# A decoder trunk in fp32: inverse square roots moved from VectorE and ScalarE to one power instruction on GpSimd

## The chip, the cores and the metric

The kernel runs on one core of a Trainium2 chip. The metric is the device time of one launch, the median of three runs. The engines that matter are TensorE (PE, matrix products; PEld is its weight load), VectorE (DVE), ScalarE (ACT), GpSimd (POOL) and SyncE (SP, which issues most DMAs). Each engine works through its own queue in order, and an instruction that waits holds up what stands behind it on that engine.

## What is computed

Two decoder layers over 256 tokens of width 2048, then a final RMS norm, all in fp32. Layer 0 has three head groups (a gated convolution, a Mamba-2 scan, an attention into 256 memory tokens), layer 1 has two (latent attention and memory attention). What the change touches is the norm that stands in many places:

```
def rms_norm(x, w):
    y = xf * lax.rsqrt(jnp.mean(xf * xf, axis=-1, keepdims=True) + EPS)
    return (y * w.astype(jnp.float32)).astype(x.dtype)

mem_n = rms_norm(mem, mem_norm_w)
h = rms_norm(x, norm_w)                                        # both layers
y_b = y_b * lax.rsqrt(jnp.mean(y_b * y_b, axis=-1, keepdims=True) + EPS)   # layer 0, per group
q = (rms_norm(c_q, mla_q_norm_w) @ mla_w_uq)                   # layer 1
kv = (rms_norm(c_kv, mla_kv_norm_w) @ mla_w_ukv)
return rms_norm(x, final_norm_w)
```

## The kernel before

The weights stream in from HBM as a list of units; a unit is 128 or 512 output columns of one weight matrix. Each weight chunk of 128x1024 is split into a high and a low part: ScalarE casts the high part (`wh_...`, L160), VectorE subtracts it to get the low part (`wl_...`, L161), and TensorE multiplies both with activations that are split in the same way. L381 are products with a high part, L376 those with a low part; the low ones of a unit run together with those of its neighbour. L391 to L393 are the same for token-major units such as `wv`, and L627 for the packed units `dt` and `kr` (whose parts both lie in `wh_kr`, made by ScalarE in L146 and VectorE in L147).

After its products a unit has a post function. It is a generator: it does some work, yields, and is taken up again a step of the stream later. A tile scheduler then orders the instructions of each engine by priority and by what it expects them to cost, and this order is fixed in the program. High priority is given to evictions (`ev`, L397) and splits.

The inverse roots stand in three helpers. `rsqrt` (L276) works on 128x2 values: the mean plus epsilon, a bit estimate over integers, and three Newton steps. It serves the memory norm (`rcol`, value `rmc_r`), the group norms of layer 0 (`post_z`, value `grg`) and the norm of layer 1 (`post_x1`, value `r1c`). `rbcast` spreads such a column over all partitions: a diagonal `dg` on VectorE (L309), a product with ones on TensorE (`rm_pb`, L310) and a copy on ScalarE (L312). `rfull` (L315) works on 128x256 values that are already spread (a product with ones, L320): the same steps, but with a yield ahead of each Newton step. It serves x's norm in layer 0 (`r0b`) and the norms of the q and kv ranks in layer 1 (both `rc`, the last step L342 multiplies by layer 1's own root). What follows is a product with the norm's weights (L509 `hn`, L1037 `ct`) and the split into high (L346) and low half (L347).

The memory norm's root also scales the values `vm` on ScalarE (L583) and, spread as `rm`, the keys `kT` on VectorE (L581, L594). x's squares are ScalarE's (L493, L496), VectorE adds them up (L497), GpSimd folds the sum (L498), and TensorE spreads it (`r0b_ss`). Layer 1's evictions `evr` (L1007) multiply by `st["r1"]` on GpSimd.

The final norm (`post_o`, L1262) takes ScalarE's square root with the running sum as bias, a reciprocal on VectorE and one Newton step, then scales and stores five pieces of each half.

Of the kernel before, what the change touches and what calls it, by code (L numbers as in the profile page):

```python
# [204 lines left out]
def trunk_kernel(ctx, tc, a, out):  # L205
# [69 lines left out]

    def rsqrt(ssq, n, out):  # L276

        m = ssq.shape[1]
        v = tmp("nv", "nv", 2, (P, 4))[:, :m]
        V.tensor_scalar(v, ssq, 1.0 / n, EPS, ALU.mult, ALU.add)  # L280
        f = tmp("nf", "nf", 2, (P, 4))[:, :m]
        V.tensor_copy(f, v.bitcast(I32))
        V.tensor_scalar(f, f, -0.5, 1597463007.0, ALU.mult, ALU.add)
        yi = tmp("ni", "ni", 2, (P, 4), I32)[:, :m]
        V.tensor_copy(yi, f)
        y = yi.bitcast(F32)
        for i in range(3):
            V.tensor_tensor(f, y, y, ALU.mult)
            V.scalar_tensor_tensor(f, f, -0.5, v, ALU.mult, ALU.mult)
            nxt = out if i == 2 else tmp("ny", "ny", 3, (P, 4))[:, :m]  # L290
            V.scalar_tensor_tensor(nxt, f, 1.5, y, ALU.add, ALU.mult)
            y = nxt

    def rcol(accs, n, name):

# [16 lines left out]
        A.copy(rb, pb)  # L312
        return rb

    def rfull(accs, n, name, tag="rb", bufs=2, spread=True, by=None):  # L315


        ps = pat.tile([P, T], F32, name=f"{name}_ss", tag="at")
        for k, acc in enumerate(accs):
            PE.matmul(ps, ones, acc, start=k == 0, stop=k == len(accs) - 1)  # L320
        out = tmp(name, tag, bufs)
        vf = S(f"{name}_vf")
        v, f = vf[:, 0:T], vf[:, T:2 * T]
        yi = S(f"{name}_yi", I32)[:, 0:T]
        if by is None:
            V.tensor_scalar(v, ps, 1.0 / n, EPS, ALU.mult, ALU.add)
        else:
            V.scalar_tensor_tensor(v, ps, 1.0 / n, by[1], ALU.mult, ALU.mult)
            V.tensor_scalar(v, v, EPS, None, ALU.add)
        V.tensor_copy(f, v.bitcast(I32))  # L330
        V.tensor_scalar(f, f, -0.5, 1597463007.0, ALU.mult, ALU.add)
        V.tensor_copy(yi, f)
        y = yi.bitcast(F32)
        for i in range(3):
            if spread:
# [926 lines left out]
    def post_o(g):  # L1262
        def f(ps):
            gfin, xts = st["o", g]
            for i in range(2):
                xt = xts[i]
                if g == 3:
                    pre, ph = (tmp(n, n, 2, (P, 1)) for n in ("rp", "rh"))
                    V.tensor_reduce(pre, ssq[:, i, 0:3], AX.X, ALU.add)
                    V.tensor_scalar(pre, pre, 1.0 / D, EPS, ALU.mult, ALU.add)  # L1270
                for pi, (c0, p) in enumerate(ps[i]):
                    n = slice(c0, c0 + p.shape[1])
                    V.tensor_tensor(xt[:, n], p, xt[:, n], ALU.add)
                    jk = S("jk")
                    A.activation(jk[:, n], xt[:, n], AF.Square, accum_out=ssq[:, i, g + pi:g + pi + 1])
                    if g == 3 and pi + 1 == len(ps[i]):
                        V.tensor_scalar(ph, pre, -0.5, None, ALU.mult)
                    if pi + 1 < len(ps[i]):
                        V.scalar_tensor_tensor(pre, ssq[:, i, 3:4], 1.0 / D, pre, ALU.mult, ALU.add)
                    V.tensor_tensor(gfin[i][:, n], xt[:, n], gfin[i][:, n], ALU.mult)  # L1280
                x1t[i][g] = gfin[i]
                if g == 2 and i == 1:
                    A.activation(warm, ssq[:, 1, 2:3], AF.Sqrt)
                if g == 3:
                    s_ = ssq[:, i, 2 + len(ps[i]):3 + len(ps[i])]
                    v, y, z = (tmp(n, n, 2, (P, 1)) for n in ("rv", "ry", "rz"))
                    A.activation(y, s_, AF.Sqrt, scale=1.0 / D, bias=pre)
                    V.scalar_tensor_tensor(v, s_, -0.5 / D, ph, ALU.mult, ALU.add)
                    V.reciprocal(y, y)
                    V.tensor_scalar(z, y, y, v, ALU.mult, ALU.mult)  # L1290
                    r = tmp("rr", "rr", 2, (P, 1))
                    V.tensor_scalar(r, z, 1.5, y, ALU.add, ALU.mult)
                    for gg, c0, n in ((1, 0, 256), (0, 0, 512), (1, 256, 256), (3, 0, 512), (2, 0, 512)):
                        xo = x1t[i][gg][:, c0:c0 + n]
                        if gg == 0:
# [104 lines left out]
```

## Time and profile before

| | |
|---|---|
| median of three runs | 1184.31 us (1184.0 to 1185.1) |
| the profiled execution | 1183.59 us |
| its span, from the first to the last instruction | 1181.9 us |
| TensorE, weight load | 1172.1 us busy, 1017.2 us |
| VectorE, ScalarE, GpSimd | 859.7, 666.6, 83.0 us busy |
| granted TensorE clock | full, but for the last of 40 slices (0.8) |
| read from HBM, written | 220.23 MB, 4.23 MB |

The durations in the rows come from the profiled execution. Its time is 1.7 us more than the span, and 0.7 us less than the median. In a timeline a row is the start in us, the length in us, engine, line, operation, the tile written and those read, the shape, the number of merged instructions, and in brackets the idle time of the engine ahead of it with what ended that. The length of one instruction runs until its result is there; the next independent one begins a little earlier.

### The profile page before, as it was taken

What the parts mean: (1) busy time and instruction counts of PE and PEld (TensorE: products, weight loads), DVE (VectorE), ACT (ScalarE), POOL (GpSimd) and SP (SyncE); (2) the same over time, 40 slices, a digit from 0 to 9 for tenths busy, and PEclk for the clock granted to TensorE, in tenths of its full rate; (3) what the DMA queues carried; (4) which work ended last, traced back from release to release, by engine and by line L of the source; (5) the groups of instructions that cost most, each with busy time, mean ns of one, the idle gap of its engine ahead of it and who ended that gap; (6) DMA issues with size and microseconds to landing.
All of it is one profiled execution on the core that took longest, in us unless ns stands there. A gap on an engine that the chain in (4) does not pass through costs nothing.

```text
span 1181.9 us, 17221 instructions
## 1 busy us (share of the span) xinstructions
PE 1172.1 (99%) x6455; PEld 1017.2 (86%) x6455; DVE 859.7 (73%) x1592; ACT 666.6 (56%) x1195; POOL 83.0 (7%) x92
## 2 busy tenths in 40 slices
PE   9999999999999999999999999999999999999997
PEld 7888888888888898888888888889898898888886
DVE  7798897988987796666545555588766588986555
ACT  7655656666556645445444444555555587884442
POOL 0000001112000000000000000112211110110000
PEclk9999999999999999999999999999999999999998
DMA  9745646555445455555656666544554354456672
GB/s 343 268 155 208 227 162 210 182 195 188 160 172 185 147 178 199 193 187 185 216 201 214 226 214 216 176 179 165 192 184 172 108 165 139 134 187 237 230 237 98
DMA packets 45780, 225.57 MB, mean 191 GB/s; under 512 B 5473, under 2 KB 6785, under 8 KB 23425
## 3 DMA queue, kind: packets, MB, share of 16 engines
q1 hardware_dynamic: 43200, 220.88, 53.8%
q10 hardware_dynamic: 2496, 3.60, 0.9%
q8 instruction: 50, 0.82, 0.3%
q14 instruction: 34, 0.27, 0.1%
HBM read 220.23 MB, written 4.23 MB: 190 GB/s over the span
## 4 chain that ended last, share of the span: by engine, by line
PE 94%; DVE 3%; ACT 2%; issue 1%; POOL 0%; DVEq 0%; ACTq 0%; POOLq 0%
PE ps_mm L381 32%; PE ps_mm L376 17%; PE ps_tm L391 4%; PE ps_tm L393 4%; PE ps_tm L392 4%; PE ps_x L392 4%; PE ps_x L391 4%; PE ps_x L393 4%; PE ps_o L1232 3%; PE ps_o L1234 3%; PE ps_o L1233 3%; PE ps_k L607 1%; PE ps_mm L379 1%; PE py L783 1%; PE ps_k L609 1%; PE ps_pk L627 1%
## 5 line engine op out<-in xcount | busy, mean ns | idle before, releaser
L381 PE MATMUL ps_mm<-h,wh_zc 128*128 128x512 f32 x248 | 59.0, 391 | 0.0
L381 PE MATMUL ps_mm<-h,wh_xs 128*128 128x512 f32 x248 | 58.8, 391 | 0.0
L381 PEld LDWEIGHTS ps_mm<-h,wh_xs 128*128 128x128 f32 x248 | 45.9, 188 | 9.1
L381 PEld LDWEIGHTS ps_mm<-h,wh_zc 128*128 128x128 f32 x248 | 45.8, 188 | 9.1
L161 DVE TENSOR_TENSOR wl_wo<-raw_wo_2r,wh_wo 128x1024 fp32r<-128x1024 f32 x24 | 29.4, 1225 | 31.1 <-ACT wh_wo L160 31.1
L1232 PE MATMUL ps_o<-wh_wo,yl 128*128 128x512 f32 (+1 forms) x136 | 51.6, 379 | 0.0
L161 DVE TENSOR_TENSOR wl_wo<-raw_wo_1r,wh_wo 128x1024 fp32r<-128x1024 f32 x24 | 29.4, 1225 | 30.2 <-ACT wh_wo L160 30.1
L1233 PE MATMUL ps_o<-wl_wo,yl 128*128 128x512 f32 (+1 forms) x136 | 51.2, 377 | 0.0
L1234 PE MATMUL ps_o<-wh_wo,yl 128*128 128x512 f32 (+1 forms) x136 | 51.2, 377 | 0.0
L391 PE MATMUL ps_tm<-wh_z,h 128*128 128x512 f32 x128 | 51.1, 399 | 0.0
L161 DVE TENSOR_TENSOR wl_wo<-raw_wo_3r,wh_wo 128x1024 fp32r<-128x1024 f32 x24 | 29.4, 1225 | 29.5 <-ACT wh_wo L160 29.5
L391 PE MATMUL ps_x<-wh_wo,yb 128*128 128x512 f32 x128 | 50.1, 391 | 0.0
L393 PE MATMUL ps_tm<-wh_z,h 128*128 128x512 f32 x128 | 50.0, 390 | 0.0
L392 PE MATMUL ps_tm<-wl_z,h 128*128 128x512 f32 x128 | 49.8, 389 | 0.0
L393 PE MATMUL ps_x<-wh_wo,yb 128*128 128x512 f32 x128 | 49.8, 389 | 0.0
L392 PE MATMUL ps_x<-wl_wo,yb 128*128 128x512 f32 x128 | 49.8, 389 | 0.0
L401 ACT COPY s<-ps_mm 128x256 f32<-128x256 f32 x78 | 28.9, 371 | 33.0 <-PE ps_mm L376 18.4
L160 ACT CAST wh_wo<-raw_wo_1r 128x1024 fp32r<-128x1024 f32 x24 | 25.3, 1053 | 36.1 <-PE ps_x L393 19.6
L160 ACT CAST wh_wo<-raw_wo_2r 128x1024 fp32r<-128x1024 f32 x24 | 25.3, 1053 | 35.5 <-PE ps_x L393 19.6
L161 DVE TENSOR_TENSOR wl_wo<-raw_wo_0r,wh_wo 128x1024 fp32r<-128x1024 f32 x24 | 29.4, 1227 | 21.7 <-ACT wh_wo L160 20.0
L160 ACT CAST wh_wo<-raw_wo_3r 128x1024 fp32r<-128x1024 f32 x24 | 25.3, 1053 | 34.1 <-PE ps_x L393 19.6
L1026 POOL TENSOR_TENSOR cacc<-cacc,sq 128x256 f32<-128x256 f32 x8 | 9.0, 1122 | 441.2 <-ACT sq L1025 441.2
(776 smaller groups left out, 3504.0 us busy)
## 6 DMA issues: line engine op xcount, KB each, us to landing
raw_wo_0r<-in_w_out_dram SPq DMA_DIRECT2D x12, 1024.0 KB, 4.9
raw_wo_1r<-in_w_out_dram SPq DMA_DIRECT2D x12, 1024.0 KB, 4.9
raw_wo_2r<-in_w_out_dram SPq DMA_DIRECT2D x12, 1024.0 KB, 4.9
raw_wo_3r<-in_w_out_dram SPq DMA_DIRECT2D x12, 1024.0 KB, 4.8
raw_wkv0r<-in_wkv_dram SPq DMA_DIRECT2D x12, 512.0 KB, 7.2
raw_wv1r<-in_wv_dram SPq DMA_DIRECT2D x4, 1024.0 KB, 4.8
acb<-acd SPq DMA_DIRECT2D x16, 256.0 KB, 3.3
raw_z0r<-in_w_z_dram SPq DMA_DIRECT2D x4, 1024.0 KB, 4.7
```

The costliest lines, as they stand in the source:

```text
L160: i1 = self.nc.scalar.copy(h[:, e], part)
L161: i2 = self.nc.vector.tensor_tensor(l[:, e], part, h.bitcast(F32)[:, e], ALU.subtract)
L376: PE.matmul(ps[:, 0:T], wl, self.x[k][:, 0:T], start=not self.begun, stop=stop)
L379: PE.matmul(ps[:, c], wh, self.x[k][:, c], start=False, stop=False)
L381: PE.matmul(ps, wh, self.x[k], start=not self.begun, stop=stop)
L391: PE.matmul(ps[i], h, wh, start=first, stop=False)
L392: PE.matmul(ps[i], h, wl, start=False, stop=False)
L393: PE.matmul(ps[i], l, wh, start=False, stop=last)
L401: A.copy(s1[:m], ps[:m, T:2 * T])
L1232: PE.matmul(p, h, wh[:, n], start=first, stop=False)
L1233: PE.matmul(p, h, wl[:, n], start=False, stop=False)
L1234: PE.matmul(p, l, wh[:, n], start=False, stop=last)
```

## The change

Every inverse root becomes one instruction on GpSimd: `tensor_tensor` with the operation `pow`, the value as base and a column of -0.5, read with step 0, as exponent. `rsqrt` keeps its first instruction (mean plus epsilon) and loses twelve. `rfull` keeps its first one or two and loses twelve; the power stands ahead of the three yields. The final norm keeps the sums, and the square root, the reciprocal and the Newton step go, with the early load of the root's table (`warm`). The wide working tiles are one instead of two.

```
     ident = cst.tile([P, P], F32, name="ident")
     make_identity(nc, ident)
+    mhalf = cst.tile([P, 1], F32, name="mhalf")
+    G.memset(mhalf, -0.5)
...
     def rsqrt(ssq, n, out):
-        m = ssq.shape[1]
-        v = tmp("nv", "nv", 2, (P, 4))[:, :m]
+        v = tmp("nv", "nv", 2, (P, 4))[:, :ssq.shape[1]]
         V.tensor_scalar(v, ssq, 1.0 / n, EPS, ALU.mult, ALU.add)
-        f = tmp("nf", "nf", 2, (P, 4))[:, :m]
-        V.tensor_copy(f, v.bitcast(I32))
-        V.tensor_scalar(f, f, -0.5, 1597463007.0, ALU.mult, ALU.add)
-        yi = tmp("ni", "ni", 2, (P, 4), I32)[:, :m]
-        V.tensor_copy(yi, f)
-        y = yi.bitcast(F32)
-        for i in range(3):
-            V.tensor_tensor(f, y, y, ALU.mult)
-            V.scalar_tensor_tensor(f, f, -0.5, v, ALU.mult, ALU.mult)
-            nxt = out if i == 2 else tmp("ny", "ny", 3, (P, 4))[:, :m]
-            V.scalar_tensor_tensor(nxt, f, 1.5, y, ALU.add, ALU.mult)
-            y = nxt
+        G.tensor_tensor(out, v, mhalf[:, 0:1].to_broadcast([P, ssq.shape[1]]), ALU.pow)
...
-    def rfull(accs, n, name, tag="rb", bufs=2, spread=True, by=None):
+    def rfull(accs, n, name, tag="rb", bufs=2, by=None):
...
-        V.tensor_copy(f, v.bitcast(I32))
-        V.tensor_scalar(f, f, -0.5, 1597463007.0, ALU.mult, ALU.add)
-        V.tensor_copy(yi, f)
-        y = yi.bitcast(F32)
-        for i in range(3):
-            if spread:
-                yield
-            V.tensor_tensor(f, y, y, ALU.mult)
-            V.scalar_tensor_tensor(f, f, -0.5, v, ALU.mult, ALU.mult)
-            V.scalar_tensor_tensor(out, f, 1.5, y, ALU.add, ALU.mult)
-            y = out
+        G.tensor_tensor(out, v, mhalf.to_broadcast([P, T]), ALU.pow)
+        for _ in range(3):
+            yield
         if by is not None:
             V.tensor_tensor(out, out, by[0], ALU.mult)
...
-                if g == 2 and i == 1:
-                    A.activation(warm, ssq[:, 1, 2:3], AF.Sqrt)
                 if g == 3:
                     s_ = ssq[:, i, 2 + len(ps[i]):3 + len(ps[i])]
-                    v, y, z = (tmp(n, n, 2, (P, 1)) for n in ("rv", "ry", "rz"))
-                    A.activation(y, s_, AF.Sqrt, scale=1.0 / D, bias=pre)
-                    V.scalar_tensor_tensor(v, s_, -0.5 / D, ph, ALU.mult, ALU.add)
-                    V.reciprocal(y, y)
-                    V.tensor_scalar(z, y, y, v, ALU.mult, ALU.mult)
-                    r = tmp("rr", "rr", 2, (P, 1))
-                    V.tensor_scalar(r, z, 1.5, y, ALU.add, ALU.mult)
+                    v, r = (tmp(n, n, 2, (P, 1)) for n in ("rv", "rr"))
+                    V.scalar_tensor_tensor(v, s_, 1.0 / D, pre, ALU.mult, ALU.add)
+                    G.tensor_tensor(r, v, mhalf, ALU.pow)
```

Since the scheduler lays the program out anew, other instructions change places too. The line numbers of the changed kernel are smaller by 20 in the middle of the file (L342 is L322 there, L161 stays).

The first place is the early part of ScalarE, where the memory norm ends and x's squares begin (`vm` is scaled by the root `rmc_r`, `ea` is an exponential, `xacc` the first square). Before:

```order
L496 ACTIVATE sq_725<-x_7_442 128x512
L401 COPY s_729<-ps_mm 128x256
L160 CAST wh_wk_2_0_733<-raw_wk_2r_650 128x1024
L160 CAST wh_wk_2_1024_739<-raw_wk_2r_650 128x1024
L160 CAST wh_wk_3_0_790<-raw_wk_3r_737 128x1024
L401 COPY s_786<-ps_mm 128x256
L160 CAST wh_wk_3_1024_796<-raw_wk_3r_737 128x1024
L583 ACTIVATE vm_0_140<-vm_0_140,rmc_r 128x512
L583 ACTIVATE vm_1_141<-vm_1_141,rmc_r 128x512
L312 COPY rm<-rm_pb 128x256
L489 ACTIVATE ea<-ea 128x64
```

Now:

```order
L381 COPY s_623<-ps_k_199 128x256
L563 ACTIVATE vm_0_142<-vm_0_142,rmc_r 128x512
L563 ACTIVATE vm_1_143<-vm_1_143,rmc_r 128x512
L469 ACTIVATE ea<-ea 128x64
L473 ACTIVATE xacc<-x_0_430 128x512
L476 ACTIVATE sq_694<-x_1_432 128x512
L476 ACTIVATE sq_697<-x_2_434 128x512
```

The two multiplications of `vm` and the exponential have moved from behind the squares and three splits to ahead of the first square.

The second place is VectorE at the norm of the q rank in layer 1 (`rc_v` and `rc` are its value and root, `ct` the weighted rows, `cqHL` their halves, `wl_ckv` low parts of the weights that come next). Before:

```order
L337 TENSOR_TENSOR rc_vf<-rc 128x256
L161 TENSOR_TENSOR wl_ckv_0_7602<-raw_ckv3r_7550,wh_ckv_0_7601 128x1024
L338 SCALAR_TENSOR_TENSOR rc_vf<-rc_vf 128x256
L402 TENSOR_TENSOR crkv_7540<-ps_mm,s_7595 128x256
L339 SCALAR_TENSOR_TENSOR rc<-rc_vf,rc 128x256
L161 TENSOR_TENSOR wl_ckv_1024_7608<-raw_ckv3r_7550,wh_ckv_1024_7607 128x1024
L337 TENSOR_TENSOR rc_vf<-rc 128x256
L338 SCALAR_TENSOR_TENSOR rc_vf<-rc_vf 128x256
L339 SCALAR_TENSOR_TENSOR rc<-rc_vf,rc 128x256
L342 TENSOR_TENSOR rc<-rc,r_7219 128x256
L1037 SCALAR_TENSOR_TENSOR ct<-crq_7229,cols,rc 128x256 x2
L147 TENSOR_TENSOR wh_kr_7686<-raw_krr_7605,wh_kr_7686 128x8x64
```

Now:

```order
L316 SCALAR_TENSOR_TENSOR rc_v<-rc_ss,r1sq 128x256
L382 TENSOR_TENSOR crkv_7437<-ps_mm,s_7438 128x256
L317 TENSOR_SCALAR rc_v<-rc_v 128x256
L161 TENSOR_TENSOR wl_ckv_1024_7450<-raw_ckv2r_7388,wh_ckv_1024_7449 128x1024
L322 TENSOR_TENSOR rc<-rc,r_7119 128x256
L1017 SCALAR_TENSOR_TENSOR ct<-crq_7129,cols,rc 128x256 x2
L327 TENSOR_TENSOR cqHL_7522<-ct,cqHL_7522 128x256
L327 TENSOR_TENSOR cqHL_7527<-ct,cqHL_7527 128x256
L1017 SCALAR_TENSOR_TENSOR ct<-crq_7228,cols,rc 128x256 x2
L161 TENSOR_TENSOR wl_ckv_0_7493<-raw_ckv3r_7447,wh_ckv_0_7492 128x1024
L382 TENSOR_TENSOR crkv_7437<-ps_mm,s_7486 128x256
L161 TENSOR_TENSOR wl_ckv_1024_7499<-raw_ckv3r_7447,wh_ckv_1024_7498 128x1024
```

The root is used right behind one split, and both splits of the unit `ckv3` and all of `wh_kr` now stand behind it; before, they stood between the steps.

The third place is VectorE at the norm of the kv rank (`wl_mq` and `wl_mz` are low parts of the next units, `zc` a gate, `evr` an eviction). Before:

```order
L329 TENSOR_SCALAR rc_vf<-rc_vf 128x256
L330 CAST rc_vf<-rc_vf 128x256
L331 TENSOR_SCALAR rc_vf<-rc_vf 128x256
L332 CAST rc_yi<-rc_vf 128x256
L411 SCALAR_TENSOR_TENSOR zc_7848<-zs_th,zh 128x256
L337 TENSOR_TENSOR rc_vf<-rc_yi 128x256
L338 SCALAR_TENSOR_TENSOR rc_vf<-rc_vf 128x256
L339 SCALAR_TENSOR_TENSOR rc<-rc_vf,rc_yi 128x256
L161 TENSOR_TENSOR wl_mz_0_0_7933<-raw_mz_0r_7856,wh_mz_0_0_7932 128x1024
L405 SCALAR_TENSOR_TENSOR evr<-ps_mm,s_7925 128x256
L337 TENSOR_TENSOR rc_vf<-rc 128x256
L161 TENSOR_TENSOR wl_mz_0_1024_7939<-raw_mz_0r_7856,wh_mz_0_1024_7938 128x1024
```

Now:

```order
L161 TENSOR_TENSOR wl_mq_0_1024_7741<-raw_mq_0r_7678,wh_mq_0_1024_7740 128x1024
L317 TENSOR_SCALAR rc_v<-rc_v 128x256
L391 SCALAR_TENSOR_TENSOR zc_7730<-zs_th,zh 128x256
L322 TENSOR_TENSOR rc<-rc,r_7119 128x256
L1017 SCALAR_TENSOR_TENSOR ct<-crkv_7437,cols,rc 128x256 x2
L161 TENSOR_TENSOR wl_mz_0_0_7809<-raw_mz_0r_7738,wh_mz_0_0_7808 128x1024
L385 SCALAR_TENSOR_TENSOR evr<-ps_mm,s_7801 128x256
L327 TENSOR_TENSOR ckvHL_7781<-ct,ckvHL_7781 128x256
L327 TENSOR_TENSOR ckvHL_7786<-ct,ckvHL_7786 128x256
L1017 SCALAR_TENSOR_TENSOR ct<-crkv_7567,cols,rc 128x256 x2
L391 SCALAR_TENSOR_TENSOR zc_7730<-zs_th,zh 128x256
L161 TENSOR_TENSOR wl_mz_0_1024_7815<-raw_mz_0r_7738,wh_mz_0_1024_7814 128x1024
```

The instruction that reads the root (L342, now L322) stood behind both splits of `mz` and the first of `zc`; now it stands ahead of the first split of `mz`.

Elsewhere: on TensorE `rm_pb` has moved ahead by a unit, behind the low products of `wk_0`, and `r0b_ss` by four products; on VectorE the five multiplications of keys by `rm` and an eviction have moved in between the adds of x's squares. The order on SyncE's queue is the same.

## Rows read from the trace of the kernel before

**Rows 1.** The page: busy us (share) and instructions; the chain that ended last, by engine.

```profile
PE 1172.1 (99%) x6455; PEld 1017.2 (86%) x6455; DVE 859.7 (73%) x1592; ACT 666.6 (56%) x1195; POOL 83.0 (7%) x92
...
PE 94%; DVE 3%; ACT 2%; issue 1%; POOL 0%; DVEq 0%; ACTq 0%; POOLq 0%
```

**Rows 2.** Groups of instructions on GpSimd: name, shape, count | busy us, mean ns | idle.

```profile
L1051 POOL TENSOR_TENSOR uqrr<-rop,rop 128x256 f32<-128x256 f32 x8 | 5.9, 737 | 15.4 <-DVE rop L1048 15.4
L790 POOL TENSOR_TENSOR xsd<-xsd,yo 128x512 f32<-128x512 f32 x4 | 5.3, 1336 | 13.2 <-DVE yo L788 13.2
```

**Rows 3.** Timeline of ScalarE, 51 to 65 us: start, length, what.

```profile
51.28 0.64 ACT L493 ACTIVATE xacc<-x 128x512 f32<-128x512 f32 x1
...
62.85 1.33 ACT L583 ACTIVATE vm<-vm,rmc_r 128x512 f32<-128x512 f32 x2 [0.31 <-DVE rmc_r L291]
64.09 0.36 ACT L312 COPY rm<-rm_pb 128x256 f32<-128x256 f32 x1
```

**Rows 4.** Timeline of VectorE, 52 to 66 us.

```profile
52.69 0.68 DVE L497 TENSOR_TENSOR xacc<-xacc,sq 128x512 f32<-128x512 f32 x1
...
58.76 0.68 DVE L497 TENSOR_TENSOR xacc<-xacc,sq 128x512 f32<-128x512 f32 x1
...
64.51 0.42 DVE L326 TENSOR_SCALAR r0b_vf<-r0b_ss 128x256 f32<-128x256 f32 x1
64.85 1.42 DVE L581 TENSOR_TENSOR kT<-kT,rm 128x256 f32<-128x256 f32 x4
```

**Rows 5.** Timeline of GpSimd, 41 to 61 us.

```profile
41.40 1.65 POOL L479 TENSOR_TENSOR macc<-macc 128x256 f32<-128x256 f32 x1 [10.86 <-DVE macc L477]
59.58 1.68 POOL L498 TENSOR_TENSOR xacc<-xacc 128x256 f32<-128x256 f32 x1 [16.52 <-issue]
```

**Rows 6.** Timeline of TensorE, 57 to 74 us.

```profile
57.59 5.40 PE L381 MATMUL ps_mm<-memHL,wh_wk 128*128 128x512 f32 x23
63.35 0.68 PE L310 MATMUL rm_pb<-dg,ones 128*128 128x128 f32 x4 [0.36 <-DVE dg L309]
63.87 0.60 PE L320 MATMUL r0b_ss<-xacc,ones 128*128 128x256 f32 x2
...
70.23 3.59 PE L381 MATMUL ps_mm<-memHL,wh_wk 128*128 128x512 f32 x15
73.66 0.39 PE L391 MATMUL ps_tm<-wh_wv,memHL 128*128 128x512 f32 x1
```

**Rows 7.** Timeline of VectorE at the kv norm, 804 to 810 us.

```profile
804.11 1.71 DVE L161 TENSOR_TENSOR wl_mq<-raw_mq_0r,wh_mq 128x1024 fp32r<-128x1024 f32 x1
805.75 0.28 DVE L329 TENSOR_SCALAR rc_vf<-rc_vf 128x256 f32<-128x256 f32 x1
...
808.52 1.22 DVE L161 TENSOR_TENSOR wl_mz<-raw_mz_0r,wh_mz 128x1024 fp32r<-128x1024 f32 x1
```

**Rows 8.** Timeline of VectorE at the q norm, 774 to 787 us.

```profile
774.40 0.42 DVE L328 SCALAR_TENSOR_TENSOR rc_vf<-rc_ss,r1sq 128x256 f32<-128x256 f32 x1
...
784.29 0.42 DVE L342 TENSOR_TENSOR rc<-rc,r 128x256 f32<-128x256 f32 x1
784.75 0.88 DVE L1037 SCALAR_TENSOR_TENSOR ct<-crq,cols,rc 128x256 f32<-128x256 f32 x2
785.55 0.68 DVE L147 TENSOR_TENSOR wh_kr<-raw_krr,wh_kr 128x512 fp32r<-128x512 f32 x1
786.15 0.75 DVE L347 TENSOR_TENSOR cqHL<-ct,cqHL 128x256 fp32r<-128x256 f32 x2
```

**Rows 9.** Timeline of TensorE, the products with `kr` and the low ones with `mz`.

```profile
790.87 3.82 PE L627 MATMUL ps_pk<-h,wh_kr 128*128 128x512 f32 x16
...
811.63 2.08 PE L376 MATMUL ps_mm<-h,wl_mz 128*128 128x256 f32 x16
```

**Rows 10.** Timeline of VectorE behind the last matmul.

```profile
1175.10 0.16 DVE L1288 SCALAR_TENSOR_TENSOR rv<-ssq,rh 128x1 f32<-128x1 f32 x1
...
1176.18 1.41 DVE L1298 TENSOR_SCALAR gf<-gf,rr 128x256 f32<-128x256 f32 x4
```

More of the change, by code (lines that the diff above doesn't have):

```diff
@@ L321, in rfull @@
         out = tmp(name, tag, bufs)
-        vf = S(f"{name}_vf")
-        v, f = vf[:, 0:T], vf[:, T:2 * T]
-        yi = S(f"{name}_yi", I32)[:, 0:T]
+        v = S(f"{name}_v")[:, 0:T]
         if by is None:
@@ L1267, in f @@
                 if g == 3:
-                    pre, ph = (tmp(n, n, 2, (P, 1)) for n in ("rp", "rh"))
+                    pre = tmp("rp", "rp", 2, (P, 1))
                     V.tensor_reduce(pre, ssq[:, i, 0:3], AX.X, ALU.add)
@@ L1275, in f @@
                     A.activation(jk[:, n], xt[:, n], AF.Square, accum_out=ssq[:, i, g + pi:g + pi + 1])
-                    if g == 3 and pi + 1 == len(ps[i]):
-                        V.tensor_scalar(ph, pre, -0.5, None, ALU.mult)
                     if pi + 1 < len(ps[i]):
```

## The prediction, made before the changed kernel was run

> **What bounds the kernel now.** I began with the busy times: TensorE is busy for 99% of the span, VectorE for 73%, ScalarE for 56% and GpSimd for 7% [rows 1]. The chain that ended last agrees: 94% of it is TensorE [rows 1]. So work taken off VectorE buys nothing by itself; only what makes TensorE wait, or what stands behind its last matmul, counts. In the timeline TensorE waits visibly for one thing that the change touches, the diagonal of the memory norm: its issue would have come at 57.59 + 23 x 0.229 = 62.86 (the pace is that of 15 matmuls from 70.23 to 73.66) and came at 63.35 [rows 6], so 0.5 us. Behind the last matmul the chain of the final norm runs from 1175.10 to 1176.18 [rows 10]. These two places, 1.6 us, are all that the change can win.
>
> **What it removes.** Each of the six short roots (`rsqrt`) loses 12 VectorE instructions, each of the three wide ones (`rfull`) 12, and the tail 8. All of it but the two places above lies beside a saturated TensorE: value 0. What hides it is TensorE's own work, and that cover stays.
>
> **What it adds.** Eleven powers on GpSimd: three of 128x256, six of 128x2, two of 128x1. No row shows a power. The nearest are GpSimd's two-input passes: 737 ns for 256 columns and 1336 ns for 512 [rows 2], so 599 ns per 256 columns and 138 ns fixed. One bound is a single pass, 0.74 us. The other: a power is a logarithm, a product and an exponential; the logarithm that this kernel writes out (lines 647 to 656) takes 18 instructions, an exponential taken as long makes 36 steps, and 0.138 + 36 x 0.599 = 21.7 us. I take 12 steps, the number that the removed chain needs for the same root: 0.138 + 12 x 0.599 = **7.3 us** for a wide power, and 0.2 us for a short one. That lies nearer to the pass than to the series, and it is the weakest number here.
> [...]
>
> **What it moves.** The built order was laid out as if the power were short, and this decides the price: the waiting instruction stands early in an in-order queue, with work for TensorE behind it.
>
> *Early, x's norm.* The two multiplications of `vm` now stand ahead of the squares: these begin 1.33 us later [rows 3], VectorE's adds at 52.69 + 1.33 = 54.0 [rows 4]. Up to the last add VectorE now runs 7 adds of 0.69, six 128x256 steps of about 0.36 (four times `kT` by `rm`, and two more) and one split of 1.22 [rows 4, 7]: 8.2 us, so 62.2. GpSimd's own add ends 0.14 + 1.68 later [rows 4, 5]: 64.0. TensorE's sum `r0b_ss` stands four matmuls earlier and `rm_pb` (0.52) now ahead of it: 62.86 - 4 x 0.229 + 0.52 = 62.5 [rows 6]. It waits 1.5, against the 0.5 that `rm_pb` no longer waits (VectorE makes its diagonal ahead of the adds now, and its turn comes behind a whole unit's low products). Since VectorE overlaps instructions by some hundredths, the net is +0.6 to +1.1; **+0.9**. The wide power after it begins near 64.0 + 0.6 + 0.4 + 0.1 = 65.1 (the distance from 63.87 to 64.51 and the length of L326 [rows 4, 6]) and ends at 72.4. The first `hn` (0.5) and the split `wl_wv_0` (1.22) follow: 74.2. TensorE wants the split one matmul behind 73.66, which is 74.8 after the delay. **0**; above 8 us of power it costs the excess.
>
> *The q norm.* Value ready at 774.40 + 0.42 + 0.36 + 0.28 = 775.5 [rows 7, 8], power until 782.9. Behind it on VectorE, before the first half of `wh_kr` is done: L342 0.46, three pairs of `ct` at 0.88, three pairs of low halves at 0.75, two splits of 1.22, one eviction 0.36 and the half itself 0.68 [rows 7, 8]; 8.8 us, less some overlap, plus two hand-overs to ScalarE's casts of about half a microsecond. So about 792, where TensorE wants it at 790.87 [rows 9]. **+1.0**; it begins at 6.3 us of power.
>
> *The kv norm.* Here VectorE has least ahead. Value ready at 805.75 + 0.28 = 806.03 [rows 7], hand-over 0.14, power, then L342 0.46, two `ct` 0.80 and the split `wl_mz_0_0` 1.22 [rows 7, 8]: 808.7 plus the power. TensorE wants it at 811.63 [rows 9]. Slack 2.9 us, so a wait of 7.3 - 2.9 = 4.4. The second half of that split now has an eviction, two low halves, two `ct` and a `zc` ahead of it: 0.36 + 0.75 + 0.88 + 0.36 + 1.22 = 3.6 [rows 4, 7, 8], some 3.3 with the overlap, while TensorE eats the first in half of 2.08 [rows 9]. Another 2.3. **+6.7**. In the kernel before the same split was ready at 809.7, behind only part of the chain; the steps were spread so that none of them blocked it.
>
> *Short powers in the middle.* In the four group norms VectorE waits about 0.4 us ahead of a split, where one is prepared well before its use: 0. In layer 1's norm TensorE's broadcast also stands earlier than before, a few matmuls behind the value: 0, and the excess if a short power costs over half a microsecond.
>
> *Tail.* The square root, reciprocal and two steps go; from 1175.10 [rows 10]: 0.16 for `rv`, 0.14 hand-over, 0.17 power, 0.03 back, so 1175.6 instead of 1176.18: **-0.6**. If a short power were as slow as GpSimd's slowest pass here, 1.68 [rows 5], it would be +0.9. ScalarE's table load for the root goes too; it was hidden: 0. The DMA queues keep their order.
>
> **Sum.** +0.9 + 0 + 1.0 + 6.7 - 0.6 = +8.0 us. The profiled execution took 1183.59 with a span of 1181.9, which makes 1191.6; the median of the three runs lies 0.7 above it, 1184.31, which makes **1192.3**. At one pass per power: +0.9 - 0.6 = +0.3, 1184.6. At 21.7 us: 0.9 + 13.7 + 15.4 + 21.1 - 0.6 = +50.5, 1235. A split beside a busy GpSimd took 1.71 instead of 1.22 [rows 7]; if every power slowed VectorE so, the early place could add 1 to 3 us.
>
> **Rivals.**
> 1. *The power is short, under 4 us: not slower.* The kv slack of 2.9 us covers nearly all of it, and the early wait and the shorter tail cancel: 1184.6, up to 1186.5 near 4 us. For it: a pass costs 0.74 [rows 2]. Against it: a root to full accuracy in five passes or less, where the removed chain needed 12. Chance 0.28.
> 2. *The power is a long series or runs nearly element by element, over 14 us.* All three places then pay nearly in full: from 1184.31 + 27 = 1211 at 14 us, 1235 at 21.7, 1260 at 30 and beyond. Chance 0.20.
> 3. *The first power pays once.* It is that of the memory norm, and ScalarE's `vm` multiplications and with them all squares wait for it. [...] Against it: GpSimd's first pass of the program, like its second, shows 1.7 us and no such stretch [rows 5]. Chance 0.06. [...]
> 4. *Faster.* The early sum comes in time after all and the tail shortens: -0.5 - 0.6 = -1.1, 1183.2. More cannot come, since TensorE has no other wait to lose. Faster by over 0.2% would need twice that. Chance 0.03.
>
> **How the numbers follow.** A difference of 0.2%, 2.4 us, is about what a measurement of this kernel can tell from none. The forecast (a power of 4 to 14 us) has 0.43, and gives 1186.5 to 1211. Slower: 0.43 + 0.20 + 0.06, less 0.01 at the 4 us edge, 0.68. Same: 0.28 + 0.01, and 0.01 of rival 4, 0.30. Faster: 0.02. The range goes from 1184.0, which leaves out the lower part of rival 1 and rival 4, to 1240, a power of about 23 us, which leaves out the far part of rival 2: together about 0.17.
>
> **What would show it.** GpSimd's rows for the new line `rfull` writes with: 7 us each, and under 0.3 us for the short ones. VectorE idle ahead of `rc` with GpSimd as releaser, about 7 us at both places of layer 1. TensorE: waits at the low products of `mz` after 811 (4.4 and 2.3), at `wh_kr` (1.0) and at `r0b_ss` (1.5), none at `rm_pb`. A wide power under 3 us, or over 14, makes the number wrong and leaves the places right; a wait of TensorE anywhere else makes the reasoning wrong.

## The result: 117 us slower, and the profile after

The changed kernel takes 1301.19 us (median of five runs, 1299.19 to 1302.07) against 1184.31: a ratio of 1.098, interval 1.0966 to 1.0993. The forecast was 1192.3 with a range up to 1240, so the sign was right and the size wrong by a factor of fifteen. The span of the profiled execution grew from 1181.9 to 1298.3 us, by 116.4.

The page of the changed kernel: busy times, granted clock in 40 slices, and the chain that ended last.

```profile
PE 1178.7 (91%) x6455; PEld 1021.8 (79%) x6455; DVE 838.0 (65%) x1476; ACT 666.6 (51%) x1191; POOL 207.9 (16%) x104
...
PEclk9967999999999999999999999776699999999999
...
PE 82%; POOL 10%; DVE 3%; ACT 2%; issue 1%; DMA 1%; POOLq 0%; DVEq 0%; ACTq 0%
```

Against [rows 1], VectorE has lost 21.7 us of work and GpSimd has gained 124.9. TensorE is as busy as before but for 6.6 us, and stands still for 8% more of a longer span. GpSimd, 0% of the chain before, is now 10% of it: 125 us in three pieces. Among the longest pieces of that chain (start, length, what) they stand out:

```profile
65.39 41.27 POOL r0b L318
...
811.26 42.11 POOL rc L318
879.90 41.25 POOL rc L318
```

One power of 128x256 takes 41.3 us, the second of them 42.1. The prediction took 7.3; the upper of its two bounds was 21.7, and its second rival was priced up to 30. Why the second one is longer is not shown by a run of its own. It began 0.1 us behind the start of a split on VectorE (811.14 to 812.37), while at the beginning of the other two no split was running. The short ones, by groups of instructions on GpSimd (form, count | busy, mean ns | idle before):

```profile
L282 POOL TENSOR_TENSOR grg<-nv,mhalf 128x2 f32<-128x2 f32 x4 | 2.8, 708 | 26.5 <-DVE nv L281 26.5
L1264 POOL TENSOR_TENSOR rr<-rv,mhalf 128x1 f32<-128x1 f32 x2 | 1.1, 560 | 119.8 <-DVE rv L1263 119.8
L282 POOL TENSOR_TENSOR rmc_r<-nv,mhalf 128x2 f32<-128x2 f32 x1 | 0.7, 729 | 7.4 <-DVE nv L281 7.4
```

What TensorE waited for in the changed kernel (total us, times, longest):

```profile
PE ps_mm L356 <- DVE wl_mz L161: 41.7, 2, 40.0
PE ps_mm L361 <- ACT wh_ckv L160: 33.0, 1, 33.0
PE ps_tm L372 <- DVE wl_wv L161: 33.0, 1, 33.0
PE r0b_ss L310 <- POOL xacc L478: 1.1, 1, 1.1
PE ps_pk L607 <- DVE wh_kr L147: 1.1, 1, 1.1
```

The three large waits belong to the three wide powers, one each. VectorE reads the root, waits for it, and holds up a split behind it:

```profile
65.56 2.77 DVE L161 TENSOR_TENSOR wl_wk<-raw_wk_3r,wh_wk 128x1024 fp32r<-128x1024 f32 x2
106.69 0.48 DVE L489 SCALAR_TENSOR_TENSOR hn<-x,cols,r0b 128x256 f32<-128x256 f32 x1 [38.36 <-POOL r0b L318]
107.09 1.22 DVE L161 TENSOR_TENSOR wl_wv<-raw_wv1r,wh_wv 128x1024 fp32r<-128x1024 f32 x1
```

At the q norm the split that TensorE misses first is ScalarE's. ScalarE's queue holds the cast of `cqHL`, which needs VectorE's `ct`, ahead of the second cast of `ckv3`:

```profile
812.09 1.05 ACT L160 CAST wh_ckv<-raw_ckv3r 128x1024 fp32r<-128x1024 f32 x1 [0.65 <-PE ps_mm L361]
854.37 0.80 ACT L326 CAST cqHL<-ct 128x256 fp32r<-128x256 f32 x2 [41.23 <-DVE ct L1017]
855.08 1.04 ACT L160 CAST wh_ckv<-raw_ckv3r 128x1024 fp32r<-128x1024 f32 x1
```

So one slow instruction blocks three queues in turn: GpSimd's, VectorE's (41.0 us) and ScalarE's (41.2). TensorE here works on weights that are already split for 11.9 us from the start of the power, then stands until 2.8 us behind its end: 42.1 - 11.9 + 2.8 = 33.0.

After each of these waits TensorE is also slower. Stretches of the changed kernel (from:to, length, busy us and instructions of PE, PEld, DVE, ACT, POOL, granted clock, DMA share, GB/s):

```profile
108.36:111.87 3.51, 3.51 (x8) 2.82 (x9) 3.44 (x8) 1.00 (x3) 0.00 (x0) 0.52 0.30 65
111.87:116.00 4.13, 4.13 (x20) 3.39 (x19) 4.13 (x10) 2.90 (x6) 0.00 (x0) 1.00 0.48 198
...
923.70:926.00 2.30, 2.08 (x8) 1.78 (x8) 2.30 (x6) 1.53 (x3) 0.84 (x1) 0.50 0.00 0
926.00:929.60 3.60, 2.09 (x10) 2.09 (x10) 3.60 (x6) 2.14 (x5) 0.00 (x0) 0.50 0.33 57
```

Behind the 33 us at `wl_wv` the granted clock is 0.52 (108.36 to 111.87), and eight products take 3.51 us instead of 8 x 0.229 = 1.83: 1.7 us. TensorE at the other two places:

```profile
856.17 3.53 PE L361 MATMUL ps_mm<-h,wh_ckv 128*128 128x512 f32 x8 [33.04 <-ACT wh_ckv L160]
859.54 2.06 PE L356 MATMUL ps_mm<-h,wl_ckv 128*128 128x256 f32 x16
...
923.71 2.08 PE L356 MATMUL ps_mm<-h,wl_mz 128*128 128x256 f32 x8 [39.98 <-DVE wl_mz L161]
927.51 2.08 PE L356 MATMUL ps_mm<-h,wl_mz 128*128 128x256 f32 x8 [1.72 <-DVE wl_mz L161]
...
933.80 3.80 PE L361 MATMUL ps_mm<-h,wh_zc 128*128 128x512 f32 x16
```

At the q norm eight products take 859.54 - 856.17 = 3.4 instead of 1.83, at a granted clock of 0.53 (856.20 to 859.50): 1.5 us. At the kv norm, at 0.50 up to 929.6 and 0.72 from there to 932, it is 10.1 us from the first low product of `mz` to the next unit, of which 1.7 is the second wait. Before, it was 5.6, from 811.63 [rows 9] to this row of the same view:

```profile
817.21 1.07 PE L381 MATMUL ps_mm<-h,wh_zc 128*128 128x512 f32 x4
```

That leaves 2.8 us for the clock. The account: waits of 33.0 + 33.0 + 1.1 + 41.7 = 108.8, clock 1.7 + 1.5 + 2.8 = 6.0, `r0b_ss` 1.1, less the 0.4 that `rm_pb` no longer waits [rows 6] and 0.25 in the tail. That is 115.3 of the 116.4 us.

This account says how TensorE spent its time, not what a full clock would have given back. VectorE finishes the first half of `wh_kr` at 862.65, and its work from the root on waits for TensorE nowhere:

```profile
861.96 0.69 DVE L147 TENSOR_TENSOR wh_kr<-raw_krr,wh_kr 128x512 fp32r<-128x512 f32 x1
```

So at full clock TensorE would have been 1.5 us earlier at `wh_kr` and would have waited 1.5 us longer there. In the same way the first eight low products of `mz`, 2.08 us instead of 1.04, fill 1.0 us of the time until the second half of the split is there. By these rows, and no run tests it with the clock held up, the slow clock itself costs about 1.7 + 1.8 = 3.5 us; the other 2.5 belong to VectorE's path.

The tail, VectorE behind the last product: from `rv` to the first scaling 1292.62 - 1291.79 = 0.83 us, where it was 1.08 [rows 10].

```profile
1291.79 0.16 DVE L1263 SCALAR_TENSOR_TENSOR rv<-ssq,rp 128x1 f32<-128x1 f32 x1
1292.62 1.41 DVE L1270 TENSOR_SCALAR gf<-gf,rr 128x256 f32<-128x256 f32 x4 [0.67 <-POOL rr L1264]
```

### The profile page after: what moved, and what is told of

It is laid out like the page before. It is cut to its first block, busy times and chain, and to the rows that moved or that the text cites. A ratio compares the mean times of both kernels' runs of the same rounds, so it can differ in the third digit from the quotient of the medians.

```text
span 1298.3 us, 17105 instructions
## 1 busy us (share of the span) xinstructions
PE 1178.7 (91%) x6455; PEld 1021.8 (79%) x6455; DVE 838.0 (65%) x1476; ACT 666.6 (51%) x1191; POOL 207.9 (16%) x104
## 4 chain that ended last, share of the span: by engine, by line
PE 82%; POOL 10%; DVE 3%; ACT 2%; issue 1%; DMA 1%; POOLq 0%; DVEq 0%; ACTq 0%
PE ps_mm L361 27%; PE ps_mm L356 15%; POOL rc L318 6%; PE ps_tm L372 4%; PE ps_tm L371 4%; PE ps_tm L373 4%; PE ps_x L372 4%; PE ps_x L371 4%; PE ps_x L373 4%; POOL r0b L318 3%; PE ps_o L1212 3%; PE ps_o L1214 3%; PE ps_o L1213 3%; PE ps_k L587 1%; PE ps_mm L359 1%
## 5 line engine op out<-in xcount | busy, mean ns | idle before, releaser
L318 POOL TENSOR_TENSOR rc<-rc_v,mhalf 128x256 f32<-128x256 f32 x2 | 83.3, 41670 | 5.2 <-DVE rc_v L317 5.2
L356 PE MATMUL ps_mm<-h,wl_mz 128*128 128x256 f32 x128 | 18.7, 302 | 41.7 <-DVE wl_mz L161 41.7
L741 POOL TENSOR_TENSOR m<-m,cbT 128x512 f32<-128x512 f32 x16 | 22.7, 1423 | 211.1 <-ACT m L738 137.7
L322 DVE TENSOR_TENSOR rc<-rc,r 128x256 f32<-128x256 f32 x2 | 0.9, 426 | 82.0 <-POOL rc L318 82.0
L356 PEld LDWEIGHTS ps_mm<-h,wl_mz 128*128 128x128 f32 x128 | 17.6, 208 | 42.4 <-DVE wl_mz L161 42.2
L161 DVE TENSOR_TENSOR wl_wo<-raw_wo_2r,wh_wo 128x1024 fp32r<-128x1024 f32 x24 | 29.4, 1225 | 31.0 <-ACT wh_wo L160 31.0
L161 DVE TENSOR_TENSOR wl_wo<-raw_wo_1r,wh_wo 128x1024 fp32r<-128x1024 f32 x24 | 29.4, 1225 | 30.2 <-ACT wh_wo L160 30.1
L161 DVE TENSOR_TENSOR wl_wo<-raw_wo_3r,wh_wo 128x1024 fp32r<-128x1024 f32 x24 | 29.4, 1225 | 29.6 <-ACT wh_wo L160 29.6
```

Of the source, the lines that this page charges most:

```text
L161: i2 = self.nc.vector.tensor_tensor(l[:, e], part, h.bitcast(F32)[:, e], ALU.subtract)
L318: G.tensor_tensor(out, v, mhalf.to_broadcast([P, T]), ALU.pow)
L356: PE.matmul(ps[:, 0:T], wl, self.x[k][:, 0:T], start=not self.begun, stop=stop)
L741: G.tensor_tensor(m4, m4, cb.unsqueeze(1).to_broadcast([P, 2, 2, P]), ALU.mult)
```

## Experiments

The theory after this profile (A): a power on GpSimd costs by its columns, 0.41 us and 0.15 to 0.16 for each (an estimate from 0.56 us for one column, 0.71 for two and 41.3 for 256), and the three of 256 columns, with the queues behind them, make the whole loss. Rivals: the short powers and the new order cost something of their own (B); the place of the waiting instructions matters, not the length of the power (C); a busy GpSimd slows VectorE or TensorE (E).

### The wide roots back on VectorE, and the wide roots alone

The first kernel is the changed one with the old `rfull`; the second is the kernel before with the new `rfull` only.

```
-        G.tensor_tensor(out, v, mhalf.to_broadcast([P, T]), ALU.pow)
-        for _ in range(3):
-            yield
+        V.tensor_copy(f, v.bitcast(I32))
...
+        for i in range(3):
+            if spread:
+                yield
+            V.tensor_tensor(f, y, y, ALU.mult)
...
```

> The changed kernel, with the three wide roots back as Newton steps on VectorE; the eight short powers and the tail stay. Theory A (the three 41 us powers of 128x256, 161 ns per column, and the queues held behind them make the whole loss): the 117 us go, 1184.0 to 1184.6, the tail 0.2 to 0.3 us shorter (rv to first gf 0.83 instead of 1.08 us). Rival B (the short powers, 0.56 to 0.73 us each, and the new order of the program cost something of their own): 1186 or more, with new TensorE waits at rm_pb, at the broadcast of r1c or at the group norms.

Measured: 1184.33 us against 1184.67 for the kernel before on the same chip, ratio 0.9997 (0.9989 to 1.0006).

> The kernel before, with only the three wide roots as powers on GpSimd; short roots and tail stay Newton steps. Theory A: all of the loss stands here, 1300 to 1302, with TensorE waits of 33, 33 and 40 us and no others over 2 us. Rival B: some us less than 1301, and what is missing belongs to the short powers.

Measured: 1302.37 us, ratio 1.0993 (1.0978 to 1.1008); TensorE's large waits are 41.8, 33.9 and 33.0 us, and nothing else is over 0.4 but the 1.1 at the start that stood there before. So theory A holds: the loss is that of the three wide powers, and the eight short ones with the tail cost and win nothing that the time shows. B falls.

### The wide root on two columns

The sums are taken as a column of 128x2, the power works on that, and the column is spread as the memory norm's is.

```
+        pc = pat.tile([P, 2], F32, name=f"{name}_ss", tag="at")
+        for i in range(2):
+            for k, acc in enumerate(accs):
+                PE.matmul(pc[:, i:i + 1], acc[:, i * P:(i + 1) * P], ones[:, 0:1], ...)
...
-        G.tensor_tensor(out, v, mhalf.to_broadcast([P, T]), ALU.pow)
+        G.tensor_tensor(r, v, mhalf.to_broadcast([P, 2]), ALU.pow)
...
+        out = rbcast(r, name, tag, bufs)
```

> The changed kernel, with each wide root taken on a column of 128x2 (sums by products with one column of ones) and spread afterwards by a diagonal and a product with ones, as the memory norm does. Theory A (a power costs by its columns, 0.41 + 0.15 per column): the three powers take 0.7 us, and the time is 1184 to 1186. Rival C (what costs is the place: a root on another engine's queue, waited for early in VectorE's order): over 1190, whatever the width.

Measured: 1187.13 us, ratio 1.0024 (1.0014 to 1.0033). The same three roots in the same places, by the view of that line: length in ns (least, median, most), first and last start.

```profile
L319 POOL TENSOR_TENSOR rc_r<-rc_v,mhalf x2: 699/700/701, 776.3 to 801.0; 128x2 f32<-128x2 f32 x2
L319 POOL TENSOR_TENSOR r0b_r<-r0b_v,mhalf x1: 823/823/823, 64.5 to 64.5; 128x2 f32<-128x2 f32 x1
```

41.3 us have become 0.7 to 0.8, and 114 of the 117 us are back: the width decides, and C falls as the whole cause. The time is 1.1 us above what I expected: TensorE is busy for 1173.8 us instead of 1172.1, since the column needs 18 more products than the spread value (6473 instead of 6455), and it still waits 1.1 us at `r0b_ss`. This form is slower than Newton's steps on the spread value.

### Powers that nobody reads

```
+            powers = [(P, 1), (P, 16), (P, 64), (P, 128), (P, T), (32, T), (32, 64)] if g == 0 else [(P, T)] * 2
+            for m, c in powers if g < 2 else ():
+                pw = tmp("pw", "hn", 2)[:m, 0:c]
+                G.tensor_tensor(pw, three[:m].to_broadcast([m, c]), mhalf[:m].to_broadcast([m, c]), ALU.pow)
```

> The kernel before, plus twelve powers on GpSimd of constants, read by nobody, in the stretch where GpSimd has nothing else to do: 128x1, 128x16, 128x64, 128x128, 128x256 (three times), 32x256, 32x64 with base 3 and exponent -0.5, and 128x64 with base 1, with exponent 3 and with exponent 1. Theory A: the length is 0.41 + 0.16 per column, so 2.9, 10.6, 20.8 and 41.3 us, the same for 32 partitions as for 128, and for every exponent; nobody waits, so the time is that of before, 1184 to 1185, and the splits on VectorE beside a power take 1.22 us as else. Rival E (a busy GpSimd slows VectorE or TensorE): some 270 us of powers lengthen the splits beside them, and the time goes over 1187.

Measured: 1226.96 us, ratio 1.0362 (1.0348 to 1.0376). The groups on GpSimd:

```profile
L969 POOL TENSOR_TENSOR pw<-three,mhalf 128x256 f32<-128x256 f32 x3 | 124.8, 41608 | 0.2
L969 POOL TENSOR_TENSOR pw<-three,mhalf 32x256 f32<-32x256 f32 x1 | 41.6, 41609 | 0.1
L969 POOL TENSOR_TENSOR pw<-three,mhalf 128x128 f32<-128x128 f32 x1 | 20.7, 20728 | 0.1
L973 POOL TENSOR_TENSOR pw<-ones,mhalf 128x64 f32<-128x64 f32 x1 | 10.5, 10517 | 0.1
L973 POOL TENSOR_TENSOR pw<-three,ones 128x64 f32<-128x64 f32 x1 | 10.5, 10516 | 0.1
L969 POOL TENSOR_TENSOR pw<-three,mhalf 128x16 f32<-128x16 f32 x1 | 3.6, 3568 | 0.1
L969 POOL TENSOR_TENSOR pw<-three,mhalf 128x1 f32<-128x1 f32 x1 | 0.6, 578 | 215.9 <-DVE ya L351 215.9
```

The price is (41.608 - 0.578) / 255 = 0.161 us per column, whether 128 partitions or 32 take part (41.6 us for both on 256 columns; 10.5 and 11.0 on 64), whether the base is 3 or 1, and whether the exponent is -0.5 or 1; base 3 with exponent 3 takes the same 10.5 us on 64 columns. A column of GpSimd's two-input pass costs 0.599 / 256 = 0.0023 us [rows 2], so a power is worth about 69 passes.

Rival E falls, too, as far as such powers go. While the first nine ran without a gap from 560 to 774, VectorE's splits of the output weights took what they take in the kernel before, here those of one unit, by the view of that line over 561 to 770 us in both kernels, the run with powers first:

```profile
L161 DVE TENSOR_TENSOR wl_wo<-raw_wo_1r,wh_wo x14: 1224/1225/1226, 609.3 to 645.6; 128x1024 fp32r<-128x1024 f32 x14
```

```profile
L161 DVE TENSOR_TENSOR wl_wo<-raw_wo_1r,wh_wo x14: 1224/1225/1227, 609.4 to 645.6; 128x1024 fp32r<-128x1024 f32 x14
```

So a split did not wait for a power: 1225 ns beside it and 1225 without it. These powers read one column again and again, and the powers of the changed kernel a whole tile; but there, too, the two splits at 65.56 ran to their end beside the power of 65.39 to 106.66, in 2.77 us together, where a pair takes 2.35 at 928.05.

The time was missed, by an accident that taught something: the powers began only at 560, behind a value of VectorE, and the last ended at 805.7, when layer 1's sums of squares were waiting on GpSimd. Nobody read a power, and TensorE lost 40.8 us all the same, and 1.8 more in the 16 low products behind the wait (3.7 us, 809.10 to 812.77, where 16 take 1.9 in the kernel before, 811.63 to 813.55; during the wait, from 774 to 805, the granted clock was 0.50):

```profile
PE ps_mm L380 <- DVE wl_ckv L161: 40.8, 1, 40.8
```

ScalarE's next square (the squares have two buffers) waited 48.8 us for GpSimd's sum of an earlier one, and the casts of `ckv` stood behind that square. A power costs by what is queued behind it, not only by who reads it.

### The readers moved late

```
+            tc.keep_in_program_order(V.tensor_tensor(out, out, by[0], ALU.mult))
...
-        for _ in range(3):
+        for _ in range(3 + late):
...
-CK_LAG = 3
+CK_LAG = 8
```

with `late` 12 at the q and kv norm, 0 at x's norm.

> The changed kernel, in which the instructions that read the q and the kv root are pinned twelve steps of the stream later instead of three, and the kv norm itself five steps later; their results are first used some 100 us after the root begins. The root of x's norm stays as it is. Rival C (only the place of the waiting instructions on VectorE costs): both waits of layer 1 go, about 75 us and the slow clock after them, 1221 to 1226. Theory A with GpSimd's queue (it works in order as well, and while it is at a power, layer 1's scalings by r1, the rope and the sums of squares stand behind it, ScalarE behind those and TensorE behind ScalarE): only a part is won, 1235 to 1285, and TensorE's waits move to casts of ScalarE that follow GpSimd.

Measured: 1280.4 us, ratio 1.0812 (1.0793 to 1.0832). What TensorE waited for in layer 1 (the 33.0 us behind x's norm stay), and below it ScalarE:

```profile
PE ps_mm L356 <- DVE wl_zc L161: 57.4, 2, 36.6
```

```profile
ACT zs_th L389 <- POOL zh L990: 69.1, 19, 37.5
...
ACT sq L1005 <- POOL cacc L1006: 26.8, 1, 26.8
```

VectorE no longer waits for a root in layer 1, and 20.8 us are won out of the 75.8 that were to be had there. The rest has moved to GpSimd's queue: the squares of the kv rank (26.8 us, which stops TensorE for 20.8) and the scaled gates `zh` (37.5, which stops it for 36.6) stand behind a power, ScalarE stands behind them, and the casts behind ScalarE. GpSimd serves this stage every few us (from 782 to 897 in the kernel before its longest idle time is 8.8 us), so 41 us on it find no hole.

### The size that the prediction assumed

```
-        G.tensor_tensor(out, v, mhalf.to_broadcast([P, T]), ALU.pow)
+        G.tensor_tensor(out, v, v, ALU.mult)
+        G.tensor_tensor(out[:, 0:38], v[:, 0:38], mhalf.to_broadcast([P, 38]), ALU.pow)
```

> The changed kernel with the size that my prediction assumed: each wide root is a GpSimd product over all 256 columns (0.74 us) and a power over the first 38 (0.41 + 38 x 0.161 = 6.5), 7.3 us together; 218 columns of each root hold the square of the value and not its root. If the places and the slacks of the prediction are right and only the duration was wrong: +0.9 early, nothing at hn, +1.0 at kr, +6.7 at mz's low products (4.4 and 2.3), -0.25 tail, so 1192 to 1193. If the queues behind ScalarE's casts, which the prediction did not follow, decide at this size too: 1195 or more, with a wait of TensorE at casts of ckv.

Measured: 1198.78 us, ratio 1.0124 (1.011 to 1.0138), so 14.9 us over the kernel before, not 8. The pieces took 8.1 us together at x's and the q norm and 7.2 at the kv norm. TensorE's waits and its path through `mz`:

```profile
PE ps_mm L357 <- DVE wl_mz L161: 7.7, 2, 5.9
PE ps_pk L608 <- DVE wh_kr L147: 1.8, 1, 1.8
PE r0b_ss L310 <- POOL xacc L479: 1.1, 1, 1.1
...
PE ps_tm L373 <- DVE wl_wv L161: 0.2, 1, 0.2
```

TensorE's timeline at the kv norm:

```profile
821.19 2.08 PE L357 MATMUL ps_mm<-h,wl_mz 128*128 128x256 f32 x8 [5.94 <-DVE wl_mz L161]
824.99 2.08 PE L357 MATMUL ps_mm<-h,wl_mz 128*128 128x256 f32 x8 [1.72 <-DVE wl_mz L161]
...
832.21 3.80 PE L362 MATMUL ps_mm<-h,wh_zc 128*128 128x512 f32 x16
```

The value of the kv norm on VectorE, and the stretch of TensorE behind the first wait, columns as above:

```profile
811.02 0.28 DVE L317 TENSOR_SCALAR rc_v<-rc_v 128x256 f32<-128x256 f32 x1
```

```profile
821.00:824.00 3.00, 2.08 (x8) 1.78 (x8) 3.00 (x8) 2.23 (x5) 0.84 (x1) 0.50 0.00 0
```

The places are those of the prediction, with no wait at a cast of `ckv`: ScalarE's queue decided only at the longer power (33.0 us at 42.1, none at 8.1). The waits come to 7.7 (for 6.7), 1.8 (for 1.0), 1.1 (for 1.5) and 0.2 (for 0). The largest part of what is over that is the clock: from 821.19 to 832.21 it takes 11.0 us, where the kernel before took 5.6; less the wait of 1.7 that is 3.7 us, at a granted clock of 0.50 up to 828 and 0.69 from there to 832, after a wait of only 5.9. As above, 1.0 of it fills time in which TensorE would have waited for the second half of `mz`. Behind the 1.8 us at `wh_kr` the granted clock is 1.00 (794 to 798).

The first wait is 5.9 us and not 7.2 - 2.9 = 4.3, because the value comes later. TensorE wants the low part of `mz` at 821.19 - 5.94 = 815.25, 4.2 us behind the start of L317; before it was 811.63 - 805.75 = 5.9 [rows 7, 9]. The trace shows where this comes from: ScalarE copies out the packed product `kr`, on which this chain of VectorE and GpSimd rests, 5.8 us behind its first matmul (794.18 to 800.00) and not 3.9 (790.87 to 794.72), since what stood behind the q norm's root has piled up ahead of it.

### A version that is under both

In the changed kernel `r0b_ss` waits 1.1 us. To see whether the scalings of `vm` and `kT` ahead of x's squares cause it, they were pinned behind x's norm, in the kernel with Newton's steps for the wide roots:

```
-        for k in ks:
-            V.tensor_tensor(k, k, st["rm"], ALU.mult)
-        for i in range(2):
-            A.mul(vm[0][i], vm[0][i], st["rmc"][:, i:i + 1])
         x_square()
         yield
         yield
         yield from x_norm()
+        for k in ks:
+            tc.keep_in_program_order(V.tensor_tensor(k, k, st["rm"], ALU.mult))
+        for i in range(2):
+            tc.keep_in_program_order(A.mul(vm[0][i], vm[0][i], st["rmc"][:, i:i + 1]))
```

> As the run with Newton steps for the wide roots, and the scalings of vm and kT by the memory norm's root are pinned behind x's norm instead of standing ahead of x's squares. If these scalings are what makes r0b_ss late (1.1 us in the changed kernel), that wait goes: 1183.0 to 1183.5, 0.1% under both kernels or nearly so. If the wait comes from elsewhere (the short power before the squares, GpSimd's add), it stays, 1184.3.

Measured: 1182.76 us against 1184.06, ratio 0.9990 (0.9981 to 0.9999). All waits of TensorE that are left:

```profile
PE warm_ps L243 <- DVE wz L240: 1.1, 1, 1.1
PE ps_lt L1156 <- DVE pl L1149: 0.3, 1, 0.3
```

The time is 0.2 us below the range that I gave. `r0b_ss` waits no longer, so the scalings were the cause; `rm_pb` does not wait either, as in the changed kernel. Three controls and a repetition ask which part wins. The tail's power alone, in the kernel before:

> The kernel before, with only the final norm's root as a power of 128x1. From 1.08 to 0.83 us between rv and the first scaling: 0.25 us less, 1184.1, too little to tell from no change by the time alone; my prediction had -0.6. Rival: ScalarE's square root was hidden beside VectorE's own step and the handovers to GpSimd cost as much, then 0.

Measured: 1184.18 against 1184.67, ratio 0.9995 (0.9986 to 1.0004). The place of the scalings alone, without any power:

> The kernel before, without any power, with the scalings of vm and kT pinned behind x's norm as in the run at 1182.76. If the short powers and the tail's power give that run its gain (no wait at rm_pb, 0.4 to 0.5 us, and 0.25 us in the tail): 1184.0 as before, with the wait at rm_pb still there. If the place of the scalings alone gives it: 1182.8 to 1183.3.

Measured: 1184.34 against 1183.92, ratio 1.0002 (0.9993 to 1.0011). Beside it, on the same chip, the version again:

> The same kernel as e7_scale_late, beside the control without powers on one chip: 1182.5 to 1183.3, under the kernel before by 0.05 to 0.15%.

Measured: 1182.89, ratio 0.9990 (0.9981 to 0.9999). With the late scalings, short powers without the tail's, and the tail's without the short ones:

> The kernel at 1182.8 (short powers, tail's power, scalings behind x's norm, wide roots as Newton steps) with the final norm's root back as square root, reciprocal and Newton step. If its gain comes from the short powers and the order they bring (no TensorE wait at rm_pb): 1183.0 to 1183.3, only the tail's 0.25 us given back. If it comes from the tail: 1184.0 or more.

Measured: 1183.53 against 1184.13, ratio 0.9994 (0.9985 to 1.0003), which lies between the two cases and decides for neither.

> The control without powers (1184.34) with the tail's power alone: 0.25 us less if the tail is worth what its chain shows, 1184.1, with the wait at rm_pb of 0.4 us still there; under 1183.5 if the tail gives most of the gain.

Measured: 1184.29, ratio 1.0000 (0.9991 to 1.0009); `rm_pb` waits 0.4 us there.

Only both parts together, with the late scalings, can be told from the kernel before, by 0.1%, twice, and both times the interval ends just short of 1. The short power for the memory norm takes away the wait at `rm_pb`, and the tail's chain is 0.25 us shorter; the rest of the 1.0 to 1.3 us lies within what single runs differ by, and which part gives it stays open.

## Why the prediction was wrong, and where it was right

**What failed: the price of a power.** "I take 12 steps, the number that the removed chain needs for the same root: 0.138 + 12 x 0.599 = 7.3 us for a wide power" is the step, and the 36 steps that make 21.7 are the bound above it. A wide power is worth 69 passes, and takes 41.3 to 42.1 us. Neither the removed chain nor a written-out logarithm says how GpSimd makes a power, and how it does stays open. The short one was mis-sized by the same step: 0.70 to 0.73 and 0.56 us for 0.2. The range ended at a power of 23 us, so it could not hold the result.

**What held: the places, and two of the three thresholds.** Put 41.3 us into the prediction's own sums: 41.3 - 8 = 33.3 behind x's norm, 41.3 - 6.3 = 35.0 at the q norm, 41.3 - 2.9 + 2.3 = 40.7 at the kv norm. The waits are 33.0; 33.0 and 1.1 together 34.1; and 41.7. At the assumed size a power of 8.1 us cost 0.2 behind x's norm (threshold 8) and 1.8 at the q norm (threshold 6.3). At the q norm one stop was missed, though: the prediction followed VectorE to `wh_kr`, and 33 us of the wait came earlier, through ScalarE's cast of `cqHL`, which stands ahead of a cast of `ckv3`. By its own sign ("a wait of TensorE anywhere else makes the reasoning wrong") that counts against it at this length. Its sum came out near all the same, because VectorE's path to `wh_kr` ends last of the two. With 0.9 early and the measured 0.25 in the tail the sum is 109.6 us, or 1293.9. Of the 7.3 us that are missing to 1301.2, 6.0 are products at the slow clock: about 3.5 that it cost, and 2.5 in which VectorE's path was longer than the sums say. The other 1.3 stay open.

**What was left out: the slow clock after a wait.** 6.0 us in the changed kernel, of which about 3.5 were its price, and 3.7 us in the run of the assumed size, of which 2.7 were. It is the largest single part of why that size gives 1198.8 and not 1192.3. The slack at the kv norm was also smaller than the 2.9 us of the sum: 7.2 of power made a first wait of 5.9, so 1.3 was left, since the q norm's power delays the kv norm's value as well. The three places were priced as if they were independent. And one sum at the edge is off by its own terms: near 4 us of power the kv norm costs 4 - 2.9 + 2.3 = 3.4, so rival 1 and the forecast meet at 1188.0 and not at 1186.5, which changes nothing in the outcome.

**Early.** `r0b_ss` waits 1.1 us (predicted 1.5), for the reason given: the scalings ahead of the squares. `rm_pb` waits no longer. **Tail.** -0.25 instead of -0.6, all of it the short power's 0.56 for 0.17. **Removed work at 0**: right for the short roots and the tail. With Newton's steps only in the wide roots VectorE has 10 us less to do (849.4 instead of 859.7) and the time is the same.

**Rivals.** Rival 2, a power of over 14 us, is what happened; it had 0.20 and the right three places, and its figures stopped at 30 us. Whether the power is a long series is not shown. Rival 3 falls: the first power of the program takes 0.73 us, the later ones of its shape 0.70 to 0.71. The 1.6 us named as all that could be won was not passed: the best version here wins 1.0 to 1.3.

## What to carry to other kernels

Before a chain of simple steps is replaced by one rich instruction on another engine, measure that instruction by itself at the width in which it will be used: the number of steps it replaces says nothing on its price. In this kernel a power on one or two columns (0.6 to 0.8 us on GpSimd) cost nothing that the time shows, and gained at most 0.1%; on a value that is already spread it cost 117 us. Here a power in GpSimd's in-order queue was paid by everything that was queued behind it (40.8 us of TensorE's time in the run in which nobody read one) and behind its readers (waits of 33.0, 33.0 and 41.7 us); moving the readers late helped only as far as nobody else needed that engine (20.8 of 75.8 us), and the waits of TensorE had to be priced with the slow products after them (6.0 us), less what another wait behind them took up (2.5 of the 6.0, an estimate from the rows above).

## What the runs showed of the hardware

- A power cost 0.161 us per column on 32 partitions as on 128 (41.6 us on 256 columns), and 10.5 us on 64 columns for base 1 with exponent -0.5 and for base 3 with -0.5, 1 or 3. None of these values made it faster.
- Two hundred us of powers without a gap did not slow VectorE's splits (1225 ns in both kernels), where in the kernel before a short GpSimd pass (`zh`, 0.74 us from 804.00) had gone with a split of 1.71 instead of 1.22 us [rows 7].
- After a wait of TensorE of 5.9 us its products ran at a granted clock of 0.50 (821 to 828) and 0.69 (828 to 832) and took 3.7 us more, 1.0 of them in place of waiting by an estimate from the rows; after one of 1.8 us they ran at 1.00 (794 to 798).
